# The last eight units of a neighbourhood attention take the transposing detour, and its value strips are copied in one group instead of two

## The chip, the cores and the metric

The kernel runs on one core of a Trainium2 chip. The metric is the time of one execution on the device in microseconds (us), as the median of several runs. The engines are named as the profile names them: PE is TensorE's matmul and PEld its weight load, DVE is VectorE, ACT is ScalarE, POOL is GpSimd, and SP is SyncE, which issues most of the DMAs here. A name with q (SPq, ACTq) is the engine's instruction queue.

## What is computed

One encoder layer runs over two independent sequences, one of 512 and one of 1024 tokens, with 1024 channels. In short:

```python
xn = rmsnorm(x)
z  = xn @ w_in       # q_A k_A v_A | q_B k_B v_B | gate_A gate_B
o_a = gqa_attention(rope(rmsnorm(q_A)), rope(rmsnorm(k_A)), v_A)   # 8 heads of 64, 2 key/value heads
o_b = neighbourhood_attention(q_B, k_B, v_B, rpb)                  # 8 heads of 64, window 8 rows x 16 columns
mix = (sigmoid(gate_A) * (o_a @ w_proj_a) + sigmoid(gate_B) * (o_b @ w_proj_b)) @ w_out
x = x + mix
x = x + relu(rmsnorm(x) @ w_up) ** 2 @ w_down
y = rmsnorm(x)
```

In branch B the tokens form a grid 64 columns wide (16 rows for the long sequence, 8 for the short one). A token attends to the keys of a clamped window around it, with a learned bias for each head and offset, added to the scores before the softmax.

## The kernel before

All products are made in fp32 accuracy from two rounded parts: a tensor is split into `hi`, its copy rounded by ACT to fp32r, and `lo`, the remainder, which DVE (or POOL) gets by subtracting `hi`. A product is then three matmuls (hi*hi, hi*lo, lo*hi). The helpers `split`, `mul` and `mm3` do this, so that all these matmuls have line 212 and most splits lines 199 and 206.

`run` works off one sequence: the short one first (`NB == 1`, one block of 512 tokens), then the long one (`NB == 2`). The MLP of both follows. Each `run` has these stages:

- For each of two groups `g` of four heads: phase R, the projections of branch A's heads and of branch B's values. `load_a` and `load_v` load the weights (`rawqs`, `rawkvs`, `raw_vs`) over SP into a pool of three raw buffers, and they are split. For each tile of 128 tokens TensorE makes `zs` (queries, keys and values of A, with rotary tables `rts`) and two tiles later `zvs` (the values of B), which go to the DRAM tensor `vd`. Then phase A, the attention of branch A in units of (head, block of 512 queries).
- In the long sequence phase A also copies the values in DRAM, from `vd` into four strip tensors `vst[j]`, one for each strip of 32 grid columns, two copies a unit, over SP (line 808). Before the change each group copies its own four heads, 16 copies of 256 KB in each group.
- Phase B, the attention of branch B, in 32 units of (head h, strip j), in the order `[(h, j) for h in range(8) for j in (1, 2, 0, 3)]`. Its order on TensorE is written out by hand: slot i of a loop emits the scores of unit i (`s_unit`, tile `sbs`), steps of filler work (`fill.pull`), then what is due of earlier units. While it runs, TensorE's order is pinned (`held_pe`), and some issues of the other queues are held behind named instructions (`behind`). The rest of an engine's order is chosen by a scheduler.
- Filler in phase B is first the gate of branch B (`gpss`, 128 steps of three matmuls), then from slot n - 7 = 25 the projection of branch A's output (`proj_a`, tile `ppas`, 64 steps of three matmuls). Projection A loads its weights (`raw_pas`, split into `w_pas`) and gate rows (`za`) over SP, and every four steps DVE takes a result out of PSUM (`mAs`, line 912).
- Phase G: the projection of branch B (`ppbs`), the merge, the output projection.

A unit of phase B goes like this. POOL adds the bias and the mask of its two halves (`bms`, line 1033; the strips j = 1 and 2 share theirs). TensorE makes the scores of 128 queries and 384 keys for each half. DVE adds `bms` and finds the row maximum (`sbss`, line 1053), ACT takes the exponential (line 1082), DVE inverts the sum and POOL scales (`pbs`, line 1085). The probabilities must then be transposed, so that keys lie on the partitions:

- A unit in `moved` takes a detour through DRAM. `turn` (line 1094) transposes blocks of 32 x 32 on DVE in the slot after its scores and writes them to DRAM (`tbs`), `fetch_t` reads them back rearranged (`bhs`) a slot later, both over SP, and `t_unit` splits them a slot after that (ACT line 1116, DVE line 1117). `v_unit` multiplies with the strips of values (`obs`) in the fourth slot after the scores.
- A unit outside `moved` is transposed by TensorE, six transposes of 128 x 128 (`ptbs`, line 1126), and split out of PSUM by ACT and DVE (lines 1133 and 1134, two halves each). `v_unit` comes in the second slot after the scores.

Before, `moved` holds the first 24 units of the long sequence (heads 0 to 5); heads 6 and 7 use TensorE. `prep_v` loads the strips of a head (`vss`) from `vst`, and `prep(0)` at the start of phase B those of head 0. The results of heads 6 and 7 stay on the chip (`oXs`), those of the others go through DRAM.

Of the kernel before, what the change touches and what calls it, by code (L numbers as in the profile page):

```python
# [11 lines left out]
F32 = mybir.dt.float32  # L12
# [3 lines left out]
ALU = mybir.AluOpType  # L16
# [6 lines left out]
GRID_W = 64  # L23
# [38 lines left out]
def encoder(ctx: ExitStack, tc: tile.TileContext, xs, outs, w):  # L62
    nc = tc.nc
# [355 lines left out]
    def run(tr, nxt, first):  # L419
        N, x, T, NT, NB = tr.N, tr.x, tr.T, tr.NT, tr.NB  # L420
# [4 lines left out]
        vd = dram.tile([T, 8, P], F32, name=f"vd{N}")  # L425
        vst = [dram.tile([rows // 4, 32, 4, 8, P], F32, name=f"vst{N}_{j}") for j in range(4)] if NB == 2 else None
# [102 lines left out]
        for g in range(2):  # L529
            with phase(f"phR{N}_{g}") as ph:  # L530
# [159 lines left out]
                for tt in range(NT):  # L690
# [17 lines left out]
                    op = nc.sync.dma_start(rt, w["rope"][tt * P : (tt + 1) * P])  # L708
# [51 lines left out]
            with phase(f"phA{N}_{g}") as ph:  # L760
                units = [(h, qb) for h in range(4) for qb in range(NB)]
                PP = {}

                def s_tile(u, j):
                    h, qb = u
                    nm = f"{N}_{g}_{h}_{qb}_{j}"
                    q0 = (qb * 4 + j) * P
                    lhs = qT[h % 2][:, h // 2, q0 : q0 + P]
                    s = big(f"s{nm}")[:, :T]
                    for kb in range(NB):  # L770
                        ks = slice(kb * 512, kb * 512 + 512)
                        nc.tensor.matmul(s[:, ks], lhs, kT[:, 0, ks], start=True, stop=False)
                        nc.tensor.matmul(s[:, ks], lhs, kT[:, 1, ks], start=False, stop=True)  # L773
                    nm_ = sml.tile([P, 1], F32, tag="nm", name=f"nm{nm}")
                    nc.vector.tensor_reduce(nm_, s, axis=AX.X, op=ALU.max, negate=True)  # L775
                    p = ph.tile([P, T], F32, tag="P", name=f"p{nm}", bufs=8)
                    l = sml.tile([P, 1], F32, tag="l", name=f"l{nm}")
                    nc.scalar.activation(p, s, AF.Exp, bias=nm_, accum_out=l)  # L778
                    rl = sml.tile([P, 1], F32, tag="rl", name=f"rl{nm}")
                    nc.vector.reciprocal(rl, l)  # L780
                    nc.gpsimd.tensor_scalar(p, p, rl, 1.0, op0=ALU.mult, op1=ALU.mult)  # L781
                    PP[u, j] = p

                o_of = {}

                def pv(u, kc, hi, lo):
                    h, qb = u
                    if kc == 0:
                        o_of[u] = mm(f"o{N}_{g}_{h}_{qb}")
                    o = o_of[u]  # L790
                    nc.tensor.matmul(o, vhl[:, kc, :], hi, start=(kc == 0), stop=False)
                    nc.tensor.matmul(o, vhl[:, kc, :], lo, start=False, stop=(kc == NT - 1))
                    if kc == NT - 1:
                        r0 = (g * 4 + h) * HD
                        finish_o(o, 512, oad[r0 : r0 + HD, qb * 512 : qb * 512 + 512], ph, f"A{N}_{g}_{h}_{qb}")

                for j in range(4):
                    s_tile(units[0], j)
                    fill.pull(2)
                queue = []  # L800
                LAG = 2
                for ui, u in enumerate(units):
                    h, qb = u
                    if NB == 2:
                        hs = slice(4 * g, 4 * g + 4)
                        for a in range(2 * (ui % 2), 2 * (ui % 2) + 2):
                            c0 = (0, 8, 24, 32)[ui // 2]
                            nc.sync.dma_start(
                                vst[ui // 2][:, :, a, hs, :].rearrange("k c h d -> k c (h d)"),
                                vd[:, hs, :].rearrange("(k a c) h d -> a k c (h d)", a=4, c=GRID_W)[a, :, c0 : c0 + 32],  # L810
                            )
                    if first:
                        bias_row(g * 4 + ui)
                        if g == 0 and ui == 1:
                            early["a"] = load_a(1)
                        if g == 0 and ui == 2:
                            early["v"] = load_v(1, slot)
                    nxt_u = units[ui + 1] if ui + 1 < len(units) else None
                    sdone = 0
                    for kc in range(NT):  # L820
                        pt = mm(f"pT{N}_{g}_{h}_{qb}_{kc}")
                        for j in range(4):
                            nc.tensor.transpose(  # L823
                                pt[:, j * P : (j + 1) * P], PP[u, j][:, kc * P : (kc + 1) * P], ident
                            )
                        hi = ph.tile([P, 512], F32R, tag="pth", name=f"pth{N}_{g}_{h}_{qb}_{kc}", bufs=3)
                        lo = ph.tile([P, 512], F32R, tag="ptl", name=f"ptl{N}_{g}_{h}_{qb}_{kc}", bufs=3)
                        nc.scalar.activation(hi, pt, AF.Copy)  # L828
                        nc.vector.tensor_tensor(lo, pt, hi.bitcast(F32), op=ALU.subtract)  # L829
                        queue.append((u, kc, hi, lo))  # L830
                        if nxt_u is not None:
                            while sdone < 4 and kc >= ((0, 1, 3, 4) if NB == 2 else (0, 0, 1, 2))[sdone]:
                                s_tile(nxt_u, sdone)
                                sdone += 1

                        fill.pull(1 if NB == 1 or kc % 4 < 3 else 0)
                        if len(queue) > LAG:
                            pv(*queue.pop(0))
                fill.drain()
                for item in queue:  # L840
                    pv(*item)
# [80 lines left out]
        with phase(f"phB{N}") as ph:  # L922
# [2 lines left out]
            rects, strips, bms, PT = {}, {}, {}, {}  # L925
            units = [(h, j) for h in range(8) for j in (1, 2, 0, 3)]
            n = len(units)
            moved = set(units[: n - 8]) if NB == 2 else set()

            def raw_here(name):  # L930
                if NB == 2:
# [179 lines left out]
            def t_unit(u):  # L1111
                h, j = u
                nm = f"{N}_{h}_{j}"
                if u in moved:
                    hi, lo = (PT[u][:, i].rearrange("p a f k i -> p (a f k i)") for i in range(2))
                    nc.scalar.activation(hi, lo.bitcast(F32), AF.Copy)
                    nc.vector.tensor_tensor(lo, lo.bitcast(F32), hi.bitcast(F32), op=ALU.subtract)
                    return
                pt = [mm(f"ptb{nm}_{hf}") for hf in range(halves)]

                hl = ph.tile(
                    [P, halves * nkc, 2, P], F32R, tag="bh", name=f"bh{nm}", bufs=3 if NB == 2 else 2
                )
                for hf in range(halves):
                    for i in range(nkc):
                        op = nc.tensor.transpose(  # L1126
                            pt[hf][:, i * P : (i + 1) * P], PT[u][hf][:, i * P : (i + 1) * P], ident
                        )
                        if held_pe:
                            tc.keep_in_program_order(op)  # L1130
                    src = pt[hf][:, : nkc * P].rearrange("p (k q) -> p k q", q=P)
                    dh, dl = (hl[:, hf * nkc : (hf + 1) * nkc, i, :] for i in range(2))
                    nc.scalar.activation(dh, src, AF.Copy)
                    nc.vector.tensor_tensor(dl, src, dh.bitcast(F32), op=ALU.subtract)
                PT[u] = hl
# [51 lines left out]
            for i, u in enumerate(units):  # L1187
                ls = 3 if u in moved else 3 - NB
                due_t.setdefault(i + ls, []).append(u)
                due_v.setdefault(i + ls + 1, []).append(u)  # L1190
            for i in range(n + 4 - NB):
                if moved:
                    slot_no[0] = i
                if i < n - 8:
                    f = (5 if i < 2 else 2 + i % 2) if NB == 1 else 5 - (i % 6 == 5)
                else:
                    f = 3 + i % 2 if NB == 1 else 8
                if NB == 2 and i == n - 11:
                    pa = proj_a(ph, raw_here)
                    next(pa)  # L1200
                if i < n:
                    late = i > 0 and units[i - 1] in moved
                    if i > 1 and units[i - 2] in moved:
                        fetch_t(units[i - 2])
                    s_unit(units[i], partial(turn, units[i - 1]) if late else None)
                    h, j = units[i]
                    if j == 1 and h < 7:
# [16 lines left out]
                        if i + 1 < n - 8:  # L1224
                            wqk = load_qk(i // 8 + 2, held)
                if NB == 2 and i == n - 7:
                    for u in due_v.pop(i):
                        v_unit(u)
                    fill.drain()
                    fill.add(pa)  # L1230
                fill.pull(f // 2)
# [745 lines left out]
```

## Time and profile before

| | |
|---|---|
| median of 3 runs | 2136.32 us (2136.04 to 2136.45) |
| the profiled execution | 2136.87 us, of which the span of the profile is 2135.0 us |
| mean granted TensorE clock | 0.997 |
| phases A and R of the second group, long sequence | about 452 to 782 us |
| phase B, long sequence | about 782 to 1059 us |
| first score of head 6 to first product of phase G | 987.4 to 1059.2 us |

In the rows of the profile, `out<-in` names the tiles written and read. A row of a timeline has the start, the length, the engine, the line, the operation, the tiles and a count, and in square brackets the idle time before it and what ended that. A row of the windows has the stretch, its length, the busy time of PE, PEld, DVE, ACT and POOL (with the number of instructions), the granted TensorE clock as a share of full speed, the mean busy share of the DMA engines and what they moved in GB/s. A row of an instruction group by line has the count, then its durations in ns (least, median, most) and the first and last start; a row of the costliest groups has after the count the busy time in us and the mean in ns, then the idle time before. A matmul's listed length includes its fill and drain, which overlap with the next one, so the pitch of matmuls in a row is read from their starts.

### The profile page before, as it was taken

Reading aid. Unit: us, or ns where it says so; the run is one execution under the profiler, and the core shown is the slowest. Engines: PE = TensorE matmul, PEld = TensorE weight load, DVE = VectorE, ACT = ScalarE, POOL = GpSimd, SP = SyncE. Lnnn points to the kernel's source line nnn. Section 1 sums busy time; section 2 is a strip of 40 time slices with the busy share of each in tenths; the row PEclk is TensorE's granted clock in tenths of the full one; section 3 lists DMA queues with packets and bytes.
Section 4 is the critical chain, followed back from the end, with each engine's and each line's share of the span. In section 5 each row is a group of like instructions: output and inputs, shape, how many; then the busy total and the mean of one; then the engine's idle time right before and its main releaser. Section 6 shows DMA issues by size and latency. Waiting matters only on the chain.

```text
span 2135.0 us, 31762 instructions
## 1 busy us (share of the span) xinstructions
PE 2099.9 (98%) x10871; PEld 1840.2 (86%) x10871; DVE 1483.2 (69%) x2793; ACT 1146.3 (54%) x2487; POOL 362.0 (17%) x446
## 2 busy tenths in 40 slices
PE   9999999999989999999999999999999999999998
PEld 8888778988888888888888899999999988888887
DVE  6665786767647756787882877778777777759563
ACT  6664653767556645555531556556655643434352
POOL 2232310323233314442101200003000000000000
PEclk9999999999999999999999999999999999999999
DMA  6437557520133038876472666578445799688561
GB/s 192 133 99 212 148 165 254 184 89 29 59 111 107 25 97 245 244 219 196 153 246 103 203 196 193 162 249 210 158 146 158 259 351 344 215 276 282 166 203 64
DMA packets 340072, 381.31 MB, mean 179 GB/s; under 512 B 30911, under 2 KB 267079, under 8 KB 339911
## 3 DMA queue, kind: packets, MB, share of 16 engines
q1 hardware_dynamic: 301687, 313.99, 46.9%
q10 hardware_dynamic: 31072, 45.11, 6.0%
q0 software_dynamic: 7152, 20.19, 3.5%
q8 instruction: 86, 1.41, 0.3%
q14 instruction: 75, 0.61, 0.1%
HBM read 282.68 MB, written 105.71 MB: 182 GB/s over the span
## 4 chain that ended last, share of the span: by engine, by line
PE 53%; DVE 1%; issue 0%; ACT 0%; POOLq 0%; POOL 0%; ACTq 0%; DVEq 0%
PE dn L212 20%; PE ua L212 6%; PE ud L212 6%; PE uc L212 6%; PE ops L212 4%; PE ub L212 3%; PE ppbs L212 2%; PE ppas L212 2%; PE dnf L212 2%; PE pt L353 0%; PE obs L212 0%; PE gpss L212 0%; PE sbs L212 0%; PE ptbs L1126 0%; DVE A L1452 0%
## 5 line engine op out<-in xcount | busy, mean ns | idle before, releaser
L212 PE MATMUL dn<-wd,ah 128*128 128x512 f32 x1248 | 384.3, 389 | 0.0
L212 PEld LDWEIGHTS dn<-wd,ah 128*128 128x128 f32 x1248 | 234.2, 188 | 48.7
L212 PE MATMUL dn<-wd,al 128*128 128x512 f32 x624 | 242.8, 389 | 0.0
L1451 ACT ACTIVATE ah<-ar 128x512 fp32r<-128x512 f32 x168 | 104.4, 628 | 206.0 <-PE dn L212 186.7
L212 PE MATMUL gpss<-xs_0h,w_gs 128*128 128x512 f32 x512 | 188.7, 402 | 0.8 <-DVE ot_Bs L472 0.4
L1452 DVE TENSOR_TENSOR al<-ar,ah 128x512 fp32r<-128x512 f32 x168 | 114.4, 687 | 75.5 <-ACT ah L1451 67.9
L212 PE MATMUL ud<-B,A 128*128 128x384 f32 x768 | 143.6, 334 | 0.7 <-DVE c L1569 0.7
L212 PE MATMUL uc<-B,A 128*128 128x384 f32 x768 | 143.7, 334 | 0.0
L212 PE MATMUL ua<-B,A 128*128 128x384 f32 x768 | 138.8, 334 | 0.0
L212 PEld LDWEIGHTS dn<-wd,al 128*128 128x128 f32 x624 | 117.1, 188 | 24.2
L781 POOL TENSOR_SCALAR ps<-ps,rls 128x1024 f32<-128x1024 f32 (+1 forms) x96 | 96.8, 1010 | 226.4 <-DVE rls L780 201.0
L212 PEld LDWEIGHTS ud<-B,A 128*128 128x128 f32 x768 | 133.9, 188 | 1.1 <-DVE c L1569 1.1
L212 PEld LDWEIGHTS uc<-B,A 128*128 128x128 f32 x768 | 134.1, 188 | 0.2 <-ACT A L1451 0.2
L212 PEld LDWEIGHTS ua<-B,A 128*128 128x128 f32 x768 | 133.7, 188 | 0.2
L829 DVE TENSOR_TENSOR ptls<-pTs,pths 128x512 fp32r<-128x512 f32 x160 | 107.7, 686 | 37.3 <-ACT pths L828 36.3
L828 ACT ACTIVATE pths<-pTs 128x512 fp32r<-128x512 f32 x160 | 94.0, 597 | 73.4 <-PE pTs L823 71.3
L212 PE MATMUL ops<-wh_os,mgs 128*128 128x512 f32 x384 | 119.4, 390 | 0.0
L775 DVE TENSOR_REDUCE nms<-ss 128x1 f32<-128x1024 f32 (+1 forms) x96 | 99.9, 1041 | 25.6 <-PE ss L773 25.1
L212 PEld LDWEIGHTS gpss<-xs_0h,w_gs 128*128 128x128 f32 x512 | 96.3, 189 | 18.9 <-DVE w_gs L206 0.7
L778 ACT ACTIVATE ps<-ss,nms 128x1024 f32<-128x1024 f32 (+1 forms) x96 | 93.2, 972 | 23.4 <-DVE nms L775 20.6
L180 POOL TENSOR_TENSOR rs_f<-ms_f,mhalf 128x1 f32<-128x1 f32 x6 | 4.0, 667 | 590.7 <-DVE ms_f L176 590.7
L823 PEld LDWEIGHTS pTs<-ident,ps 128*128 128x128 f32 x640 | 77.7, 140 | 28.6 <-POOL ps L781 4.3
(287 smaller groups left out, 5152.4 us busy)
## 6 DMA issues: line engine op xcount, KB each, us to landing
ar<-ud SPq DMA_DIRECT2D x120, 512.0 KB
br<-in_w_mlp_down_dram SPq DMA_DIRECT2D x72, 512.0 KB
rawu<-in_w_mlp_up_dram SPq DMA_DIRECT2D x64, 512.0 KB
ud<-c ACTq DMA_DIRECT2D x128, 192.0 KB
raw_gs<-in_w_in_dram SPq DMA_DIRECT2D x32, 512.0 KB
ud<-cs SPq DMA_DIRECT2D x64, 192.0 KB
tbs<-pbs SPq DMA_DIRECT2D x24, 384.0 KB
bhs<-tbs SPq DMA_DIRECT2D x24, 384.0 KB
```

What stands on the lines that cost most here:

```text
L180: nc.gpsimd.tensor_tensor(r[:, :n], m[:, :n], mhalf[:, :n], op=ALU.pow)
L212: op = nc.tensor.matmul(out, a, b, **kw)
L775: nc.vector.tensor_reduce(nm_, s, axis=AX.X, op=ALU.max, negate=True)
L778: nc.scalar.activation(p, s, AF.Exp, bias=nm_, accum_out=l)
L781: nc.gpsimd.tensor_scalar(p, p, rl, 1.0, op0=ALU.mult, op1=ALU.mult)
L823: nc.tensor.transpose(pt[:, j * P : (j + 1) * P], PP[u, j][:, kc * P : (kc + 1) * P], ident)
L828: nc.scalar.activation(hi, pt, AF.Copy)
L829: nc.vector.tensor_tensor(lo, pt, hi.bitcast(F32), op=ALU.subtract)
L1451: nc.scalar.activation(hi, src, AF.Copy)
L1452: nc.vector.tensor_tensor(lo, src, hi.bitcast(F32), op=ALU.subtract)
```

## The change

- `moved` now holds all 32 units of the long sequence. So heads 6 and 7 take the detour too.
- For these two heads the subtraction of the rounded copy in `t_unit` runs on POOL instead of DVE (128 x 768 elements, both operands in SBUF).
- From slot n - 8 on, six steps of filler a slot instead of eight. The loop of the long sequence has 36 slots instead of 34, since the last unit's product is now due in slot 35. The last unit's `turn` is called in slot 32, the fetches go on to slot 33.
- The product that was due in slot n - 7 is no longer made ahead of draining the gate, but at the end of the slot like the others.
- The strip copies run only in the second group's phase A, for all eight heads at once: 16 copies of 512 KB.

```diff
-                    if NB == 2:
-                        hs = slice(4 * g, 4 * g + 4)
+                    if NB == 2 and g == 1:
                         for a in range(2 * (ui % 2), 2 * (ui % 2) + 2):
                             c0 = (0, 8, 24, 32)[ui // 2]
                             nc.sync.dma_start(
-                                vst[ui // 2][:, :, a, hs, :].rearrange("k c h d -> k c (h d)"),
-                                vd[:, hs, :].rearrange("(k a c) h d -> a k c (h d)", a=4, c=GRID_W)[a, :, c0 : c0 + 32],
+                                vst[ui // 2][:, :, a].rearrange("k c h d -> k c (h d)"),
+                                vd.rearrange("(k a c) h d -> a k c (h d)", a=4, c=GRID_W)[a, :, c0 : c0 + 32],
                             )
...
-            moved = set(units[: n - 8]) if NB == 2 else set()
+            moved = set(units) if NB == 2 else set()
...
                     nc.scalar.activation(hi, lo.bitcast(F32), AF.Copy)
-                    nc.vector.tensor_tensor(lo, lo.bitcast(F32), hi.bitcast(F32), op=ALU.subtract)
+                    sub = nc.gpsimd if h >= 6 else nc.vector
+                    sub.tensor_tensor(lo, lo.bitcast(F32), hi.bitcast(F32), op=ALU.subtract)
                     return
...
-            for i in range(n + 4 - NB):
+            for i in range(n + 3 if NB == 1 else n + 4):
...
-                    f = 3 + i % 2 if NB == 1 else 8
+                    f = 3 + i % 2 if NB == 1 else 6
...
+                if 1 < i < n + 2 and units[i - 2] in moved:
+                    fetch_t(units[i - 2])
+                if i == n and moved:
+                    turn(units[i - 1])
                 if i < n:
                     late = i > 0 and units[i - 1] in moved
-                    if i > 1 and units[i - 2] in moved:
-                        fetch_t(units[i - 2])
                     s_unit(units[i], partial(turn, units[i - 1]) if late else None)
...
                 if NB == 2 and i == n - 7:
-                    for u in due_v.pop(i):
-                        v_unit(u)
                     fill.drain()
                     fill.add(pa)
```

## The prediction

> **What bounds the kernel now.** I read the page first, then windows for stretches where TensorE is not full, then the timelines of TensorE and of SP's queue at such a place, and last the chain and the windows of the stretch in which heads 6 and 7 run.
>
> ```profile
> span 2135.0 us, 31762 instructions
> PE 2099.9 (98%) x10871; PEld 1840.2 (86%) x10871; DVE 1483.2 (69%) x2793; ACT 1146.3 (54%) x2487; POOL 362.0 (17%) x446
> ```
>
> TensorE bounds the kernel: busy 98% of the span. So time can come only from TensorE instructions taken away, from its 35 us of idle time, and from stretches at a lower clock. The change reaches one large hole. A window (length, busy time of PE, PEld, DVE, ACT and POOL, granted clock, DMA share, GB/s) and TensorE's timeline (start, length):
>
> ```profile
> 600.00:602.50 2.50, 2.50 (x13) 2.35 (x12) 2.01 (x4) 0.67 (x1) 2.50 (x4) 0.50 0.10 29
> ```
>
> ```profile
> 593.35 0.34 PE L212 MATMUL zs<-wghs,xs_0l 128*128 128x384 f32 x1
> 599.43 0.58 PE L212 MATMUL zvs<-wh_vs,xs_0h 128*128 128x256 f32 x1 [5.74 <-ACT wh_vs L199]
> 605.68 0.38 PE L622 MATMUL pqs<-ident,rrs 128*128 128x128 f32 x2
> ...
> 610.14 0.28 PE L212 MATMUL zvs<-wh_vs,xs_0h 128*128 128x256 f32 x1
> 613.01 0.49 PE L622 MATMUL pqs<-ident,rrs 128*128 128x128 f32 x3
> ```
>
> In the projections of the second head group of the long branch TensorE waits 5.74 us for the split weights of V; then the clock stands at 0.50. At full clock the same 24 V matmuls of a later tile take 613.01 - 610.14 = 2.87 us. Why the weights were late is on SP's queue (start, length of the group of issues); below it stand VectorE's group and ACT's row for the buffers:
>
> ```profile
> 447.31 0.99 SPq L510 DMA_DIRECT2D rawkvs<-in_w_in_dram  x2
> 452.22 134.65 SPq L808 DMA_DIRECT2D vsts<-vds  x16
> 586.99 4.00 SPq L245 DMA_DIRECT2D raw_vs<-in_w_in_dram  x2
> ```
>
> ```profile
> L206 DVE TENSOR_TENSOR wgls<-rawqs,wghs x4: 665/676/1318, 467.8 to 535.9; 128x512 fp32r<-128x512 f32 x4
> 585.46 0.23 ACT L661 ACTIVATE sqs<-zs 128x64 f32<-128x64 f32 x1 [3.57 <-PE zs L212]
> ...
> 598.32 1.06 ACT L199 ACTIVATE wh_vs<-raw_vs 128x1024 fp32r<-128x1024 f32 x1 [3.29 <-DMA raw_vs<-in_w_in_dram]
> ```
>
> The 16 strip copies of the first group hold SP's queue from 452 to 587; the loads of the V weights (raw_vs) stand right behind them, and the rotary tables (rts) behind those. ACT waits for raw_vs until 598.32. The raw buffers that raw_vs needs had been free since about 537, when the last rawqs was split. So the queue order is what makes them late.
>
> The second place, heads 6 and 7: one slot of the chain, with one attention-times-V group of six matmuls from a detoured unit beside it, and two windows.
>
> ```profile
> 996.71 0.72 PE obs L212 x6
> ...
> 1035.80 0.69 PE obs L212 x4
> 1036.49 0.71 PE sbs L212 x4
> 1037.20 2.75 PE ppas L212 x12
> 1039.96 0.66 PE ptbs L1126 x6
> ```
>
> ```profile
> 1010.00:1050.00 40.00, 39.90 (x204) 33.86 (x204) 33.59 (x85) 25.79 (x51) 10.67 (x14) 1.00 0.55 166
> 930.00:950.00 20.00, 20.00 (x107) 17.64 (x106) 17.06 (x43) 12.63 (x26) 13.77 (x14) 1.00 0.88 256
> ```
>
> TensorE is full there too, so its transposes (ptbs) are on the path. The last row is a stretch where units already take the detour: TensorE is full with DVE at 17.06 of 20 and the DMA at 0.88.
>
> **The change part by part. 1, strip copies in the second group only.** The 16 copies of 256 KB at 452 to 587 go; raw_vs and rts then follow rawkvs on SP directly and wait for their own buffers alone, so raw_vs lands some 50 us before 593. ACT is idle before 585.46 (3.57 us), so the split fits ahead of the V matmuls. From the end of zs (593.35 + 0.17, one matmul's pitch) to pqs at 605.68 is 12.16 us, in which 24 V matmuls (2.87) and one of zs (0.17) run: 3.05 us of work at full clock. Gain 12.16 - 3.05 = 9.1 us, of which 5.74 is the wait and 3.4 the half clock with a small wait in it. Bounds: 9.1 if nothing is late in its place, 5.7 if something keeps a short hole, so that the clock still falls, 0 if the loads stay late. What is late next: the rotated heads of the first tile, fed by rts, which has the same new head start. I take 9.1.
>
> What it adds, in the second group: its 16 copies grow to 512 KB, and the four strip loads of head 0 lose their early place.
>
> ```profile
> 642.81 2.59 SPq L950 DMA_DIRECT2D vss<-vsts  x4
> 670.12 122.23 SPq L808 DMA_DIRECT2D vsts<-vds  x13
> 793.06 2.07 SPq L245 DMA_DIRECT2D raw_gs<-in_w_in_dram  x1
> 817.69 0.39 PE L212 MATMUL gpss<-xs_0h,w_gs 128*128 128x512 f32 x1
> 827.95 0.99 PE L212 MATMUL obs<-bhs,vss 128*128 128x256 f32 x6 [0.45 <-DVE bhs L1117]
> ```
>
> Head 0's strips lie in the first group's copies, which is why they load at 642.8; now they must wait until the last copies, issued at about 792, have landed. Their first reader is at 827.95: 35 us of cover. But SP stands in that wait, with the gate weights (793.06 now, read at 817.69) and the next bias rows behind it. From the first group raw_vs took 11.3 us from issue (586.99) to its split (598.32) behind such copies; two such times after 792 is 815, just before 817.69, with the split still to come in between. So 0, bounds 0 to 4. SP issues 16 copies fewer, and the bytes stay the same.
>
> **2, the last eight units detoured.** 8 units x 0.66 us of ptbs go; six matmuls of 256 columns for four cost 0.72 - 0.69 = 0.03 each: TensorE work falls by 8 x 0.63 = 5.0 us. Projection A stays 64 steps, six a slot. A slot falls to 0.71 + 0.72 + 6 x 2.75/4 = 5.56 us, from 7.6. The other engines must keep that pace.
>
> ```profile
> L912 DVE SCALAR_TENSOR_TENSOR mAs<-zas,ppas 128x512 f32<-128x512 f32 x16 | 10.9, 683 | 4.3 <-PE ppas L212 4.2
> L1134 DVE TENSOR_TENSOR bhs<-ptbs,bhs 128x384 fp32r<-128x384 f32 x16 | 8.2, 545 | 0.2 <-ACT bhs L1133 0.2
> L206 DVE TENSOR_TENSOR w_pas<-raw_pas,w_pas 128x256 fp32r<-128x256 f32 x12 | 6.1, 532 | 0.0
> L1094 DVE STREAM_TRANSPOSE pbs<-pbs x24: 960/965/979, 815.9 to 990.8; 128x768 f32<-128x768 f32 x24
> L1116 ACT ACTIVATE bhs<-bhs x24: 830/847/850, 825.5 to 1001.0; 128x768 fp32r<-128x768 f32 x24
> L1085 POOL TENSOR_SCALAR pbs<-pbs,rlbs 128x384 f32<-128x384 f32 x64 | 51.2, 806 | 53.8 <-DVE rlbs L1084 53.5
> L1033 POOL TENSOR_TENSOR bms<-rects,msks 128x384 f32<-128x384 f32 x48 | 44.9, 954 | 54.9 <-DVE nmbs L1053 54.6
> L365 POOL TENSOR_TENSOR B<-ta,B x12: 1283/1296/1303, 1176.4 to 1462.2; 128x512 fp32r<-128x512 f32 x12
> L365 DVE TENSOR_TENSOR B<-ta,B x12: 678/774/1370, 1179.1 to 1464.0; 128x512 fp32r<-128x512 f32 x12
> ```
>
> VectorE: 33.59/40 of a slot of 7.7 us (0.69 + 0.71 + 0.66 + 8 x 2.75/4 = 7.6, and a little more where a detoured unit's product comes in) is 6.5 us. Of that 2 x 0.545 (subtracting out of PSUM) goes, 0.965 (block transposes) comes, and two steps fewer save 0.34 (half a mAs) and 0.27 (half a w_pas pair): 5.8 us, over TensorE's 5.56. Eight slots make 1.9 us if VectorE can be always busy; at 90% busy (the row at 930 shows 85%, with TensorE as the bound) a slot is 6.4 us and eight lose 6.8. Below nothing: 0, as the detoured stretch at 930 shows with slots shorter than these (0.71 + 0.72 + five gate steps of 2.75/4, 4.9 us), and slots 32 to 35, which have no scores, leave room to catch up. I take 3.0, a little under the middle: the detoured stretch is the nearest row, and it loses nothing.
>
> GpSimd: the subtraction of 768 columns, from 1.296 for 512 and 0.954 for 384, is an estimated 1.9 us. With 2 x 0.81 and 3/4 of 2 x 0.954 a slot holds 4.9 of 5.56 us. It fits, and nothing waits for the subtraction until the product over a slot later. It is queued ahead of the next unit's mask sums, which VectorE's row maxima need. ACT: one copy of 0.847 for two out of PSUM, nothing. SP: 16 more DMAs (8 out, 8 back) of 384 KB in 65 us, beside 166 GB/s: 6.3 MB/65 us = 97, together about 263, near the 256 of the full stretch.
>
> **3, the order at the end.** The product of unit 21 goes behind the gate's last steps, nothing. The tail: the last block transposes run in slot 32, are fetched in 33, copied in 34 and used at the end of 35. Between copy and use lie seven steps and one product, 7 x 0.69 + 0.72 = 5.5 us against 0.85 + 1.9: covered by 2.7. Without that cover it costs up to 2.8.
>
> **Sum.** -9.1 - 5.0 + 3.0 = -11.1 us. The profiled execution took 2136.87 us, which gives 2125.8; it stands 0.55 above the median of 2136.32, so I say 2125.2.
>
> **A rule beside a row.** A short hole matters for the range:
>
> ```profile
> 987.41 1.28 PE L212 MATMUL sbs<-kBs,qBs 128*128 128x384 f32 x3 [1.84 <-DVE kBs L1015]
> 988.00:990.00 2.00, 2.00 (x7) 1.71 (x6) 1.91 (x5) 1.00 (x2) 0.31 (x1) 0.50 0.03 11
> ```
>
> After an idle of only 1.84 us the clock was 0.50. So a late operand in the tight slots can cost twice its length. The Trainium skill (TensorE: Matmul & The Clock Gate, "Why this matters for your kernels") asks for idle gaps above about 3 us before the clock halves; by it such a hole would cost only itself, 1.84, and here the row says otherwise.
>
> **Rivals.** (a) GpSimd's subtraction and VectorE hold each other up. VectorE's subtraction with both inputs in SBUF takes 678 to 1370 ns (L365, median 774) where GpSimd subtracts beside it: up to 0.7 us of waiting. If that comes with each of two operations a slot, VectorE's slot is 5.8 + 1.4 = 7.2 us and eight slots lose 8 x 1.64 = 13; if with one, 6.5 us and 7.5. In place of the 3.0 a loss of 7.5 to 10 gives 2136.3 - 14.1 + 7.5 to 10 = 2129.7 to 2132.2, say 2131. Against it: w_pas, the commonest such operation, is short. The Trainium skill (SBUF — State Buffer, "SBUF: two separate sides") calls the port pair that both share an exclusive lock for the whole instruction, which is this mechanism; the spread of L365 agrees.
> (b) The loads stay late: raw_vs is put on SP's queue no earlier, since it had been placed last with its buffers long free. Then part 1 brings 0: 2136.3 - 2.0 = 2134.3. Against it: rawkvs of the same group was issued at 447, a whole phase ahead.
> (c) Slower: GpSimd's order becomes a loop. Mask sums, row maximum, exponential and scaling of a unit go round in the 4.9 us of a detoured slot at most; the subtraction (1.9), which waits for ACT's copy and so for the DMA, now stands before the next unit's mask sums. Bare that is 6.8 us at most. Both the subtraction and mask sums are in slots 27 to 31, five, so it decides from 14.1/5 = 2.8 us a slot, at 8.4 us, 1.6 us of waiting in each; at 9 it gives 2136.3 - 14.1 + 5 x 3.44 = 2139.4. For it: the queue is in order, so a late fetch holds up the mask sums behind it. Against it: the bare loop is under 8.4, and one unit of four has no mask sums of its own.
>
> **How the numbers follow.** Forecast 0.63 (2121.5 to 2128.5: from all of the 14.1 and a little more, if the 1.84 us hole above closes in the new order, to VectorE's whole 6.8), (a) 0.20, (b) 0.10, (c) 0.07. The range 2121.5 to 2132.2 leaves out (b) and (c), 0.17. Within 0.2% (2132.05 to 2140.6), about what a measurement of this kernel cannot tell from no change, lie (b) and a quarter of (a), 0.15; below it the forecast and the rest of (a), 0.78; above it (c), part of which would be called no change, 0.07.
>
> **What would show it.** Right: no idle above 1 us between 581 and 620 and clock 1.00 there; raw_vs issued before 540; no ptbs in the long branch; some 5 us less from the first score of head 6 to the first ppbs, less what VectorE loses. Wrong: scores (sbs) or products (obs) waiting for bms or bhs in heads 6 and 7, windows there at clock 0.50, or a hole near 817 from gate weights behind SP's wait.

## The result, and the profile after

The changed kernel takes **2171.3 us** (median of 4 runs, 2170.6 to 2172.0) against 2136.2 (2135.9 to 2136.5): ratio 1.0164, 95% interval 1.0147 to 1.0182. It is 1.6% slower; I had forecast 2125.2. The profiled execution of it took 2171.96 us, with a span of 2170.2, 35.2 us above that of before.

From the page of the changed kernel, the span and the first of its busy lines:

```profile
span 2170.2 us, 31700 instructions
PE 2099.6 (97%) x10839; PEld 1838.2 (85%) x10839; DVE 1488.6 (69%) x2785; ACT 1142.5 (53%) x2479; POOL 379.7 (17%) x454
```

TensorE has 32 instructions fewer (48 transposes out, 16 products in, as worked out), but its time busy is what it was, and all of the 35 us is idle time. The 5.0 us of work that were taken out do not show in the time busy: the mean granted clock fell from 0.997 to 0.989, so what is left ran slower. First the place of the old hole, in the changed kernel: SP's queue from 447 us on, and the window over it:

```profile
447.36 0.99 SPq L510 DMA_DIRECT2D rawkvs<-in_w_in_dram  x2
469.86 67.16 SPq L245 DMA_DIRECT2D raw_vs<-in_w_in_dram  x2
578.18 1.29 SPq L708 DMA_DIRECT2D rts<-in_rope_dram  x3
```

```profile
590.00:610.00 20.00, 20.00 (x139) 20.00 (x138) 9.23 (x25) 12.77 (x64) 6.90 (x9) 1.00 0.22 70
```

The first of the two loads of V's weights is issued at 469.86 instead of 586.99, the second at about 537, when its buffer comes free. TensorE is full there and the clock is 1.00. This part came as forecast. The new hole is 230 us later. Below are rows of TensorE before and after: the start of phase B's query projection (pqbs), the first scores of phase B (sbs), the first scores of head 6, and the second projection (ppbs). The idle time before a row stands in brackets.

```profile
782.06 0.39 PE L212 MATMUL pqbs<-xs_0h,w_bqs 128*128 128x512 f32 x1
805.86 0.34 PE L212 MATMUL sbs<-kBs,qBs 128*128 128x384 f32 x1
...
985.24 0.34 PE L212 MATMUL sbs<-kBs,qBs 128*128 128x384 f32 x1
...
1059.00 2.25 PE L212 MATMUL ppbs<-oXs,w_pbs 128*128 128x512 f32 x9
```

```profile
776.42 0.80 PE L212 MATMUL pqbs<-xs_0h,w_bqs 128*128 128x512 f32 x1 [3.09 <-ACT w_bqs L199]
834.38 0.69 PE L212 MATMUL sbs<-kBs,qBs 128*128 128x384 f32 x1 [32.45 <-ACT kBs L1012]
...
1016.02 0.34 PE L212 MATMUL sbs<-kBs,qBs 128*128 128x384 f32 x1
...
1093.23 2.70 PE L212 MATMUL ppbs<-oXs,w_pbs 128*128 128x512 f32 x11
1096.71 3.50 PE L212 MATMUL ppbs<-oXs,w_pbs 128*128 128x512 f32 x13 [0.79 <-ACT oXs L480]
```

The table ahead gave 987.4 for the first score of head 6; that is the row behind a short idle, and the first score itself starts at 985.24. Four differences make the account. Phase A of the second group ends at 776.42 - 3.09 = 773.3 instead of 782.06: **8.7 us gained**. From there to the first scores it is 61.0 us instead of 23.8: **37.3 lost**. From the first scores to those of head 6, 181.6 instead of 179.4: 2.3 lost (another hole of 0.73 us, and a granted clock of 0.50 from 834 to 840). From there to the second projection, 77.2 with 0.8 of idle behind it instead of 73.8: **4.2 lost**. Together 35.1 of 35.2 us.

The large hole, followed back through ACT (timeline), SP's queue (timeline, lengths of groups of issues), what SP waited for between 640 and 806 us (total, times, longest), and two windows:

```profile
826.51 1.06 ACT L199 ACTIVATE w_gs<-raw_gs 128x1024 fp32r<-128x1024 f32 x1 [34.22 <-DMA raw_gs<-in_w_in_dram]
829.19 1.06 ACT L199 ACTIVATE w_gs<-raw_gs 128x1024 fp32r<-128x1024 f32 x1 [1.62 <-DMA raw_gs<-in_w_in_dram]
830.27 0.59 ACT L991 ACTIVATE qBs<-pqbs 64x512 fp32r<-64x512 f32 x1
...
833.13 1.19 ACT L1012 ACTIVATE kBs<-pkbs 64x512 fp32r<-64x512 f32 x2
```

```profile
645.21 157.36 SPq L807 DMA_DIRECT2D vsts<-vds  x16
802.69 4.68 SPq L941 DMA_DIRECT2D rects<-biases  x1
807.41 13.66 SPq L949 DMA_DIRECT2D vss<-vsts  x4
821.17 0.51 SPq L245 DMA_DIRECT2D raw_gs<-in_w_in_dram  x1
```

```profile
SPq L807 <- DMA oads<-os_As: 100.5, 4, 46.1
SPq L807 <- DMA zgs<-sgs: 31.4, 3, 15.6
```

```profile
790.00:795.00 5.00, 5.00 (x24) 4.14 (x23) 2.06 (x3) 0.84 (x2) 0.00 (x0) 1.00 0.26 106
795.00:800.00 5.00, 5.00 (x24) 4.14 (x23) 0.00 (x0) 0.00 (x0) 0.00 (x0) 1.00 0.26 106
```

Read upwards from the scores: they need the rounded keys (kBs). Those stand in ACT's queue behind the split of the gate weights, which stands 34.22 us for its load. That load was issued at 821.17 instead of 793.06, because SP had 16 strip copies, a bias row and head 0's four strip loads ahead of it. While copies run, at 790 to 800, the mean busy share of the DMA engines is 0.26 and 106 GB/s move. So a copy of 512 KB takes 5.0 us, as if on **4 of the 16 engines**. The pattern of the copies, `k c (h d)`, has k = 4 as its slowest dimension. The Trainium skill (DMA: Bandwidth & Descriptors, "Why a DMA increments its semaphore by 16 and not by 1") says that a transfer is spread over the largest number of engines up to 16 that divides the slowest dimension of both patterns, which is 4 here; the trace agrees with its share of 0.26.

The waits in the third fence are for stores of tensors that the copies do not touch. In the compiled program each transfer of SP's and ACT's queues signals one of eight semaphores (DMAHW0 to DMAHW7), which both queues use in turn, and the next transfer on a semaphore waits for the last one on it. Three copies as they stand there, with names shortened:

```
vsts_1 <- vds   [waits DMAHW1]
vsts_1 <- vds   [waits DMAHW2]
vsts_1 <- vds   [waits DMAHW3]
```

So a copy can wait for a store of phase A's output that comes tens of microseconds later. Of the 157.36 us of the copies in SP's queue 131.9 are such waits. Whether the rate or this waiting makes the hole is settled below.

### The profile page after: what moved, and what is told of

Its sections match the earlier page's. It is cut to its first block, busy times and chain, and to the rows that moved or that the text cites. A ratio compares the mean times of both kernels' runs of the same rounds, so it can differ in the third digit from the quotient of the medians.

```text
span 2170.2 us, 31700 instructions
## 1 busy us (share of the span) xinstructions
PE 2099.6 (97%) x10839; PEld 1838.2 (85%) x10839; DVE 1488.6 (69%) x2785; ACT 1142.5 (53%) x2479; POOL 379.7 (17%) x454
## 4 chain that ended last, share of the span: by engine, by line
PE 49%; DVE 2%; DMA 1%; issue 1%; ACT 0%; POOLq 0%; POOL 0%; ACTq 0%; DVEq 0%; SPq 0%
PE dn L212 19%; PE ua L212 6%; PE ud L212 6%; PE uc L212 6%; PE ops L212 4%; PE ub L212 3%; PE ppbs L212 2%; PE dnf L212 2%; PE pt L353 0%; DMA bhs<-tbs 0%; DMA rawos<-obds 0%; PE gpss L212 0%; DVE w_pas L206 0%; PE ppas L212 0%; DVE A L1452 0%
```

## The experiments

Kernels of one set were timed beside the kernel before, whose median was 2136.7 to 2137.1 us in them; the ratio is what to compare. T1, T2 and so on name the theories of the texts put on record ahead of each run.

**One part alone.** The detour with the copies as before, and the copies alone:

```diff
 # detour only: the changed kernel, with the copies of before
+                    if NB == 2:
+                        hs = slice(4 * g, 4 * g + 4)
 ...
 # copies only: the kernel before, with
+                    if NB == 2 and g == 1:
```

> Only the detour part of the change; the strip copies stay split over both groups as in the kernel before. Theory T1 (the 32 us hole before the second phase B comes from the second group's 512 KB copies, which run on 4 of the 16 DMA engines at 105 GB/s, 5 us each, and hold the queue in front of the gate weights): the hole at 834 is gone, the hole at 593 (5.7 us and the half clock behind it) is back, heads 6 and 7 take 78.2 us instead of 73.9, so 2136.2 + 4.3 = 2140.5 us (2138 to 2143). Theory T2 (the hole comes from SP standing at head 0's strip loads, because all copies are in the second group, whatever their rate): the same 2140.5 us, it is not told apart from T1 here. Theory T3 (the detour of heads 6 and 7 is the main loss, the hole only moved it): over 2150 us.

> Only the strip copies' part of the change, no detour in heads 6 and 7. T1 and T2: the gain of 8.7 us at the end of the second group's phase A and the loss of 39.5 us before the first scores both stay, so 2136.2 - 8.7 + 39.5 = 2167 us (2163 to 2170). T3: about 2127 us.

Measured: detour only 2141.4 us, ratio 1.0022 (1.0013 to 1.0031); copies only 2166.8, ratio 1.0141 (1.0126 to 1.0156). By the ratios that is +4.7 and +30.1 us, 34.8 of the 35 us: the parts add, T1's two times came, and T3 falls. The copies are the loss, and the detour loses a little by itself.

**The copies over 16 engines.** The same copies with c (32 columns) as the slowest dimension on both sides, in the changed kernel and without the detour:

```diff
-                                vst[ui // 2][:, :, a].rearrange("k c h d -> k c (h d)"),
-                                vd.rearrange("(k a c) h d -> a k c (h d)", a=4, c=GRID_W)[a, :, c0 : c0 + 32],
+                                vst[ui // 2][:, :, a].rearrange("k c h d -> c k (h d)"),
+                                vd.rearrange("(k a c) h d -> a c k (h d)", a=4, c=GRID_W)[a, c0 : c0 + 32],
```

> The changed kernel with the same 16 copies of 512 KB at the same places, but the access patterns of both sides written with c (32 columns) as the slowest dimension instead of k (4 blocks). T1: the copies spread over all 16 DMA engines, DMA share near 1 while one runs instead of 0.25, SP's issues of copies no longer take 4.6 to 7.6 us, gate weights are asked for before 800 instead of 821, no hole over 3 us before the first scores: 2171.3 - 39.5 = 2132 us (2130 to 2135). T2: the copies are as many bytes in the same place in the queue and the strip loads still wait for the last of them; most of the hole stays, over 2150 us.

> The kernel before with only the strip copies in the second group, and these with c as the slowest dimension; no detour in heads 6 and 7. T1: the gain of the first half without the hole: 2136.2 - 8.7 = 2127.5 us (2126 to 2130). T2: over 2146 us. Beside the c-first form of the changed kernel it gives the price of the detour in heads 6 and 7: 4.3 us by the two traces.

Measured: 2130.8 us, ratio 0.9972 (0.9961 to 0.9983), and without the detour 2127.0, ratio 0.9954 (0.9937 to 0.9970). The hole is gone; TensorE's first scores and SP's queue in the c-first form of the changed kernel:

```profile
797.84 0.34 PE L212 MATMUL sbs<-kBs,qBs 128*128 128x384 f32 x1
798.67 0.80 PE L212 MATMUL sbs<-kBs,qBs 128*128 128x384 f32 x3 [0.49 <-DVE kBs L1014]
```

```profile
646.15 62.85 SPq L807 DMA_DIRECT2D vsts<-vds  x16
709.10 15.55 SPq L949 DMA_DIRECT2D vss<-vsts  x4
749.10 9.33 SPq L245 DMA_DIRECT2D raw_gs<-in_w_in_dram  x2
```

The gate weights are asked for 72 us earlier. T1 gave both times within 1.3 us, and T2's (over 2150 and over 2146) did not come. But the copies also got other places among phase A's stores: SP waits 44.4 us for these here, against 131.9. So this pair doesn't tell the rate from the place.

**Nothing moved, only the pattern.** The kernel before, 32 copies in both groups, with c slowest:

> The kernel before with its 32 copies of 256 KB left in both groups, only c as their slowest dimension. Theory T7 (the 5.7 us hole of TensorE at 593 in the kernel before comes from the rate of the copies, 2.5 us each on 4 engines in front of the value weights' loads): gone, 2128 us (2126 to 2130). Theory T8 (it comes from their place: they wait in the queue for values that are written late, whatever their rate): the hole stays, 2134 to 2137 us.

Measured 2127.6 us, ratio 0.9955 (0.9940 to 0.9970): T7's time came, and T8's did not. SP's queue in the first group, whose same 16 copies took 134.65 us before, and what SP waited for at these copies in the kernel before (total, times, longest):

```profile
453.32 13.84 SPq L808 DMA_DIRECT2D vsts<-vds  x16
486.57 51.51 SPq L245 DMA_DIRECT2D raw_vs<-in_w_in_dram  x2
```

```profile
SPq L808 <- DMA zgs<-sgs: 109.1, 5, 59.6
SPq L808 <- DMA oads<-os_As: 15.5, 3, 9.3
```

So the whole gain of part 1 is to be had without moving a copy, and the old hole and the new one both go with the pattern. T7's mechanism, the rate, is not shown by that. Before, 124.6 of the 134.65 us were waits for stores of the gate (zgs) and of phase A's output (oads). With the new pattern the scheduler gave the copies other places among those stores, and 3.3 us of such waits are left. How much of the old hole is the rate and how much the place was not separated.

**Smaller copies.** The changed kernel with its copies cut in two by heads (256 KB, k slowest as before), and cut in four by columns (128 KB, with c, 8 long, slowest); the copies themselves are left out of the code here:

```diff
 # halves
+                            for hs in (slice(0, 4), slice(4, 8)):   # k slowest, 32 copies
...
 # eight
+                            for c1 in range(0, 32, 8):              # c slowest, 8 long, 64 copies
...
```

> The changed kernel with each of its 16 copies of 512 KB cut in two by heads (32 copies of 256 KB, all in the second group), k still the slowest dimension. T1 (what counts is that 8 MB go over 4 engines at 105 GB/s): nothing is gained, DMA share 0.25 while they run, 2171 us (2168 to 2174). Rival T9 (a copy of 512 KB is what is too large, the 256 KB ones of the kernel before were not): the hole goes, about 2132 us.

> The changed kernel with each copy cut in four by columns (64 copies of 128 KB in the second group) and c, now 8 long, as the slowest dimension. T1: 8 engines, DMA share 0.5 and about 210 GB/s while only copies run, 40 us in all instead of 80; the hole before the first scores goes or is under 4 us: 2132 us (2129 to 2137). Rival T10 (it is the c-first order of addresses or the place in the queue that matters, not the number of engines): share near 1 as with 32 columns, or the four times larger number of issues makes SP late, over 2140 us.

Measured: halves 2179.6 us, ratio 1.0201 (1.0182 to 1.0219); eight 2157.4, ratio 1.0098 (1.0084 to 1.0112). The hole of the halves, and a window and SP's queue of the eight:

```profile
821.47 0.80 PE L212 MATMUL pqbs<-xs_0h,w_bqs 128*128 128x512 f32 x1 [37.10 <-ACT w_bqs L199]
```

```profile
795.00:800.00 5.00, 5.00 (x24) 4.15 (x23) 0.00 (x0) 0.00 (x0) 0.00 (x0) 1.00 0.51 206
```

```profile
646.16 156.57 SPq L808 DMA_DIRECT2D vsts<-vds  x64
...
807.08 0.51 SPq L245 DMA_DIRECT2D raw_gs<-in_w_in_dram  x1
```

The size of a copy is not it: T9 falls. But T1's 2171 was missed too, by 8 us; in the halves the hole stands one step earlier, ahead of the query projection. With 8 the share is 0.51 and 206 GB/s, twice that of 4: the rate follows the slowest dimension. Of the time T1 was wrong again. A hole of 18.11 us stood before the first scores, and T10's time (over 2140) came: the 64 copies were still being issued at 802, with 112.5 us of waits for stores among them. That the number of issues is the reason is not shown. One thing can be read from it beside the changed kernel, whose copies end at the same 802: the bias row and the strip loads behind them took SP 0.37 and 3.73 us here, 4.68 and 13.66 there, so the gate weights were asked for 14 us earlier, and the kernel is 14 us faster. What the rate is worth at one place, the next pair tells.

**Same place, two rates.** The copies held back by a small write that needs the fifth unit's stored output, so that SP's own queue has the same order in both:

```diff
+                    if NB == 2 and g == 1 and ui == 6:
+                        r0 = 6 * HD
+                        for j in range(4):
+                            nc.sync.dma_start(vst[j][0, 0, :, 0, :], oad[r0 : r0 + 4, 0:P])
...                      # then all 16 copies, c slowest or k slowest
```

> The changed kernel with its 16 copies of 512 KB held until the output of the fifth unit of the second group's phase A has been stored (about 735 us), by four copies of 2 KB from that output into the strips' tensors, which the 512 KB copies overwrite; c is the slowest dimension (16 engines). The c-first form without the hold had all its copies issued at 709. T1 (the rate decides): from 735 on, 16 copies at 1.3 us each, and the queue is free again by 775: no hole over 3 us, 2131 us (2129 to 2136). Theory T15 (the place in SP's queue decides: copies that wait for the stores of phase A hold the gate weights, whatever their rate): a hole of 10 us and more before the first scores, 2142 us or more.

> The same held kernel with k as the slowest dimension (4 engines), the same order of SP's queue. T1: 16 copies at 5.0 us from 735 on end at 815, 12 us later than in the changed kernel (803), 2183 us (2175 to 2190). T15: within 4 us of its c-first form.

Measured: c slowest 2140.6 us, ratio 1.0015 (1.0005 to 1.0025); k slowest 2179.4, ratio 1.0198 (1.0178 to 1.0218). One window of each while the first copies run, c first, then k; then SP's load of the gate weights and TensorE's first scores, first with c slowest, then with k:

```profile
740.00:750.00 10.00, 10.00 (x56) 8.30 (x55) 6.90 (x12) 6.48 (x13) 2.25 (x2) 1.00 0.77 224
```

```profile
740.00:750.00 10.00, 10.00 (x57) 8.32 (x56) 6.90 (x11) 6.08 (x13) 2.24 (x2) 1.00 0.27 97
```

```profile
791.25 0.49 SPq L245 DMA_DIRECT2D raw_gs<-in_w_in_dram  x1
805.66 0.69 PE L212 MATMUL sbs<-kBs,qBs 128*128 128x384 f32 x1 [2.32 <-ACT kBs L1016]
```

```profile
830.21 0.55 SPq L245 DMA_DIRECT2D raw_gs<-in_w_in_dram  x1
843.42 0.69 PE L212 MATMUL sbs<-kBs,qBs 128*128 128x384 f32 x1 [40.96 <-ACT kBs L1016]
```

The windows have waits in them; from 745 to 750 alone, where the copies' queue moves nearly all bytes, the c-first share is 1.00 at 297 GB/s, against 0.26 at 106. At the same place in SP's queue the pattern is worth 2179.4 - 2140.6 = **39 us**, which is also how much earlier the gate weights are asked for. Nearly all of it is the rate: the copies' waits for stores are not quite alike, 26.1 us with c slowest and 31.3 with k, which leaves about 34. The place has a price of its own: the held c-first form is 9.8 us slower than the free one (2130.8), its last copy being issued at 784 instead of 709. T1's 2183 for k slowest came, but its 2131 for c slowest missed those 10 us. T15 forecast a hole of 10 us with c slowest, where 2.32 stood, and a like time for both, and missed the 39. Both count, the rate three to four times as much.

**Heads 6 and 7.** The c-first form of the changed kernel costs 3.7 us more than the one without the detour. Its variants: the subtraction on VectorE; on VectorE over 64 of 768 columns; on GpSimd twice; head 6 alone detoured, with VectorE's subtraction and seven steps a unit; and VectorE's subtraction with five steps a unit.

```diff
-                    sub = nc.gpsimd if h >= 6 else nc.vector
-                    sub.tensor_tensor(lo, lo.bitcast(F32), hi.bitcast(F32), op=ALU.subtract)
+                    nc.vector.tensor_tensor(lo, lo.bitcast(F32), hi.bitcast(F32), op=ALU.subtract)
 # thin:   over lo[:, :64], hi[:, :64] for h >= 6
 # twice:  a second sub.tensor_tensor(...) for h >= 6
 # head 6: moved = set(units[: n - 4]); f = 7
 # five:   f = 5
```

> The c-first form of the changed kernel, the subtraction in heads 6 and 7 on VectorE instead of GpSimd. Theory T4 (the 3.7 us that the detour costs there come from GpSimd: while it runs its 1.9 us subtraction, VectorE's SBUF-to-SBUF instructions stand, 7.9 us in all over the 8 subtractions by the grouped rows): VectorE's own 8 subtractions at 0.96 us are 7.7 us in place of these 7.9, so 2130.8 us, 2129 to 2132.5. Theory T5 (the cost is the detour's longer way, four slots behind the last scores with two DMA trips, and VectorE has nothing to do with it): 2130.8 us as well. Theory T6 (GpSimd's queue is what is late, the masks and the scaling behind the subtractions): about 2127 us.

> The c-first form of the changed kernel, the subtraction in heads 6 and 7 on VectorE over 64 of the 768 columns only; the low parts of the other columns are left out of the computation as low parts (the whole copy stands in their place). VectorE has neither its own 0.96 us a unit nor the standing. T4: the idle stretches of TensorE in the last slots (5.0 us) and most of the half clock behind them go, 2123.5 us (2122 to 2126). T5: they stay, 2129.5 to 2131 us.

> The c-first form of the changed kernel with head 6 on the detour (subtraction on VectorE) and head 7 turned on TensorE, projection A seven steps a unit. The way behind the last scores is two slots again instead of four. T4: TensorE saves 4 x 0.63 = 2.5 us against no detour (2127.0), VectorE has 4 x 0.96 us more in slots that have room for it: 2125 us (2124 to 2127.5). T5: the same, since the tail is short again. Over 2128 us speaks against both.

> The c-first form with all units detoured and VectorE's subtraction (2128.5 us), projection A five steps a unit instead of six, so that 9 of its 64 steps are left for the end of the loop. Theory T11 (the detour's gain is lost at its end, where the last four units have no scores beside them and the last output's way through ScalarE and VectorE has nothing to cover it, 3.2 us idle ahead of the second projection): the left steps cover it, 2125.5 us (2124 to 2127). Rival T12 (VectorE sets the pace over the whole stretch, whatever the split of steps): 2128 to 2130 us.

> The c-first form of the changed kernel, with GpSimd's subtraction in heads 6 and 7 done twice over (so the low part is what is left after taking the rounded copy off two times, which is not the reference's). GpSimd has room for it: 8 x 1.9 = 15 us in a stretch where it is busy 36 of 80. T4 (VectorE's SBUF-to-SBUF instructions stand while GpSimd runs): another 4 to 8 us of standing on VectorE, which is busy 70 of 80 there, 2133 us or more (2132 to 2138), and stretched VectorE rows ending where GpSimd's ends. Rival T5 (only the way through the DMA and the tail count): 2130.8 us, at most 2131.5.

Measured:

| variant | us | ratio to before | 95% interval |
|---|---|---|---|
| GpSimd's subtraction (c-first) | 2130.8 | 0.9972 | 0.9961 to 0.9983 |
| VectorE's subtraction | 2128.5 | 0.9960 | 0.9945 to 0.9975 |
| thin | 2128.1 | 0.9956 | 0.9941 to 0.9971 |
| GpSimd twice | 2135.8 | 0.9998 | 0.9989 to 1.0007 |
| head 6 alone | 2132.7 | 0.9978 | 0.9969 to 0.9988 |
| VectorE's, five steps | 2127.0 | 0.9956 | 0.9942 to 0.9970 |
| no detour (c-first) | 2127.0 | 0.9954 | 0.9937 to 0.9970 |

In the changed kernel itself, GpSimd's, VectorE's and TensorE's rows at one of the last slots:

```profile
1075.52 1.97 POOL L1117 TENSOR_TENSOR bhs<-bhs 128x768 fp32r<-128x768 f32 x1
```

```profile
1075.14 2.63 DVE L206 TENSOR_TENSOR w_pas<-raw_pas,w_pas 128x256 fp32r<-128x256 f32 x2 [0.25 <-ACT w_pas L199]
1077.69 0.67 DVE L472 TENSOR_TENSOR ot_Bs<-obs,ot_Bs 64x512 f32<-64x512 f32 x1
```

```profile
1078.42 5.99 PE L212 MATMUL ppas<-oXs,w_pas 128*128 128x512 f32 x18 [2.48 <-DVE ot_Bs L472]
```

Two splits that take VectorE 0.73 us elsewhere take 2.63, and end 0.3 us after GpSimd's subtraction; the drain of the product (ot_Bs) stands behind them, TensorE behind that, for 2.48 us. Its 18 matmuls then take 5.99 us, with a granted clock of 0.50 from 1080 to 1083, against 4.27 at 1057.78 in the same trace. One grouped row each over heads 6 and 7, GpSimd's subtraction, VectorE's, and GpSimd's twice (count, busy us, mean ns):

```profile
L206 DVE TENSOR_TENSOR w_pas<-raw_pas,w_pas 128x256 fp32r<-128x256 f32 x14 | 10.3, 782 | 1.5 <-ACT w_pas L199 1.5
```

```profile
L206 DVE TENSOR_TENSOR w_pas<-raw_pas,w_pas 128x256 fp32r<-128x256 f32 x14 | 6.1, 462 | 0.0
```

```profile
L206 DVE TENSOR_TENSOR w_pas<-raw_pas,w_pas 128x256 fp32r<-128x256 f32 x14 | 12.0, 900 | 3.7 <-ACT w_pas L199 3.5
```

Doubling GpSimd's work cost 5.0 us, as T4 said (4 to 8), and VectorE's splits grew with it. But T4 made the two places of the subtraction equal, and VectorE's is 2.3 us better by the medians (the intervals overlap); and taking nearly all of the subtraction off VectorE brings nothing more (2128.1 against a forecast of 2123.5). So standing is not the rest of the loss. T5, the longer way at the end, would explain that rest, but not the doubling. T6's 2127 and the 2128.5 of VectorE's form cannot be told apart by their intervals, but its mechanism hardly shows: in heads 6 and 7 of the c-first form TensorE waits 0.2 us for GpSimd, and VectorE not at all. T11: leaving nine steps for the end closes the holes at the start of the second projection (3.2 to 0.2 us) and ends at 2127.0, at the edge of its range and outside T12's; against VectorE's form with six steps the intervals overlap. It equals the form without the detour, so even then the 5.0 us of TensorE's work are not gained. Where they stay is seen in that run, behind the last scores (1015.82):

```profile
1026.41 0.96 PE L212 MATMUL obs<-bhs,vss 128*128 128x256 f32 x6 [1.92 <-issue]
...
1040.87 1.00 PE L212 MATMUL obs<-bhs,vss 128*128 128x256 f32 x6 [1.10 <-DVE bhs L1116]
```

```profile
1024.98:1034.98 10.00, 8.31 (x40) 6.79 (x41) 9.88 (x19) 5.39 (x9) 0.52 (x1) 1.00 0.83 263
```

Without scores a slot of TensorE is shorter, VectorE is full (9.88 of 10), and one product waits 1.10 us for its operand; for the 1.92 us before another the profile names no cause. Head 6 alone speaks against both theories: it ended 5 us above the upper end of its range. Its trace has five holes of TensorE of 0.2 to 1.3 us between 1015 and 1031, where the products of detoured units (due four slots on) and of the others (two slots on) fall into the same slots; that this seam is the cause is read from the trace and was not tried.

## Why the prediction was wrong, step by step

- **Part 1, the gain: right.** 9.1 forecast, 8.7 measured. The loads came early, the split fitted, and the clock stayed at 1.00. Rival (b) falls.
- **Part 1, what it adds: wrong, and this decides.** The step is "So 0, bounds 0 to 4"; it was 37.3 + 2.3 = 39.6 us. Three things in it failed. The transfer time was taken from a load ("11.3 us from issue to its split") instead of from the copies' own rows: 5.0 us each at a share of 0.26. In the kernel before the smaller ones stood 134.65 us in the queue; I read that as a matter of which group they are in; the prediction uses neither their pattern nor what SP waited for. The copies were taken as issued by 792; they took SP to 802.6, and bias row and strip loads took it on to 821.17. And I followed the gate weights to their matmul only, when ACT's queue has the rounding of the queries and keys behind their split, and so the scores. The prediction's own sign, a hole from gate weights behind SP's wait, is what came, 17 us on. None of the rivals had it: the longest time among them was 2139.4.
- **Part 2, the loss of 3.0: too small, and in the wrong place.** Scores of the c-first form follow each other at 5.55 to 5.57 us in the steady slots (5.56 forecast), so VectorE does not set the pace there. In the changed kernel two of five such slots are longer (6.87 and 6.25 us), with waits for VectorE of 0.95 and 0.29 us in them: 2.0 us. But the stretch lost 4.2 us where I had -5.0 + 3.0 = -2.0; the loss term is 9.2 instead of 3.0, and above the 6.8 of its bounds. The sentence that failed is "slots 32 to 35, which have no scores, leave room to catch up". In the changed kernel it is 30.6 us from the last scores (1062.62) to the second projection. The work in it is an estimated 23.6 us, by the pitches of the prediction (0.71 for scores, 0.72 for a product, 2.75 for four steps). So about 7 us are lost there. Without the detour (c-first) the same count, with 0.69 for a product and 0.66 for six transposes, gives 15.1 us, and 15.1 were measured. Most of the 7 us show in the first two of these rows, taken from the c-first form, where the stretch is 30.8 us: 1.35 and 2.47 of idle time and 1.7 of slow clock (5.98 against 4.25 at 1042.36).

```profile
1026.67 0.96 PE L212 MATMUL obs<-bhs,vss 128*128 128x256 f32 x6 [1.35 <-issue]
1035.82 5.98 PE L212 MATMUL ppas<-oXs,w_pas 128*128 128x512 f32 x18 [2.47 <-DVE ot_Bs L472]
1054.31 1.90 PE L212 MATMUL ppbs<-oXs,w_pbs 128*128 128x512 f32 x6 [0.99 <-ACT oXs L480]
```

- **Part 3, "covered by 2.7": right for what it is said of.** In the changed kernel the last product (1092.50) waits for nothing. The way of its result through ACT, 0.8 us of idle time in the second projection (0.99 in the last row above), was not in the sum.
- **GpSimd's time: right** (1.9 us estimated, 1.91 mean over eight). **Rival (a): its mechanism is there**, 2.63 us for 0.73 of work and 5.0 us for a doubling, and it stands ahead of the longest wait; but by the medians leaving it out is worth 2.3 (subtraction on VectorE) to 2.7 us (hardly any) of the 9.2, not the 7.5 to 10 that I gave it. The Trainium skill's exclusive lock (SBUF — State Buffer, "SBUF: two separate sides") agrees with VectorE's rows that end with GpSimd's. **Rival (c)** does not show: neither scores nor row maxima wait for mask sums in heads 6 and 7.
- **Open:** which part of the 7 us at the end is the longer way and which VectorE's load. No variant got under the 2127.0 us of the form without the detour.

## What to carry to other kernels

Ahead of moving a slow DMA, ask why it is slow: read the DMA share while only it runs, and what its queue waits for. Here a share of 0.26 went with a slowest dimension of 4, and writing the 32-long dimension first, with no byte moved elsewhere, gave all of the gain (2127.6 us against 2136.7). When loads move behind others in a queue, follow each one through its splitting engine's queue to everything that stands there, not to its own reader alone. The offload to GpSimd brought nothing here, since VectorE's SBUF-to-SBUF work at that moment stood behind it. And the longer pipeline gave back at its end what it saved in its slots: count the work of the last slots for every engine, too.

## What the runs showed of the hardware that I had not expected

- DRAM-to-DRAM copies with a slowest dimension of 4, 8 and 32: DMA share 0.26, 0.51 and 1.00, and 106, 206 and 297 GB/s. SP itself stands behind such copies: the issue of one bias load took it 4.68 us in the changed kernel and 0.37 us in the form with a slowest dimension of 8.
- Transfers of different queues are tied by the semaphores that they share: in the changed kernel copies waited 131.9 us in all for stores that have nothing to do with them. No run changed the semaphores alone, so their price is not known. That a late place costs even fast copies 9.8 us was made by a hold, not by them.
